# All adaLN products of a two-layer decoder moved to TensorE, in four column tiles

## The chip, the cores and the metric

One core of one Trainium2 chip runs the whole program. The metric is device time in microseconds (us), the median of the runs shown. The engines are named as in the profile: PE (TensorE; PEld is its weight load), DVE (VectorE), ACT (ScalarE), POOL (GpSimd) and SP (SyncE, which here only issues DMAs). They run side by side, each through its own instructions in order, and wait for each other by semaphores.

## What is computed

Two layers over a sequence of 512 tokens of width 1024, in float32. Each layer is a mixer (eight heads of stick-breaking attention and four heads of gated linear attention, with one input and one output projection) and a mixture of 32 experts, two for each token. Before each of the two sub-layers stands a normalisation with a shift and a scale, behind it a gate. All six vectors of a layer come from the conditioning vector `c`:

```python
c_act = jax.nn.silu(c)                                   # (1, 1024)
for l in range(DEPTH):                                   # DEPTH = 2
    mod = (c_act @ w_ada[l] + b_ada[l])[:, None, :]      # w_ada[l]: (1024, 6 * 1024)
    shift_m, scale_m, gate_m, shift_f, scale_f, gate_f = jnp.split(mod, 6, axis=-1)
    h = rms_norm(x, norm_mix[l]) * (1.0 + scale_m) + shift_m
    x = x + gate_m * hybrid_mixer(h, ...)
    h = rms_norm(x, norm_ffn[l]) * (1.0 + scale_f) + shift_f
    x = x + gate_f * hierarchical_moe(h, ...)
```

`c_act @ w_ada[l]` is a product of one row with a matrix of 24 MB. It is what the change is about.

## The kernel before

**Stages.** Mixer of layer 0, its experts (`moe`), mixer of layer 1, its experts. A planner orders the instructions of every engine from the order in which the code makes them and from what is ready; instructions made with `kept_dma` or `tc.keep_in_program_order` keep the order of the code among themselves.

**The mixer.** Its work is a list of 80 `steps`: eight projections of eight steps each (`sb_qk(0)`, `sb_v(0)`, `sb_qk(1)`, `sb_v(1)`, `gla_qk(0)`, `gla_vr(0)`, `gla_qk(1)`, `gla_vr(1)`: steps 0 to 63) and the output projection (`out_project`, `op` in the profile: steps 64 to 79). A step has three parts: `load` (SP loads weights of two steps into a `raw` slot, six steps ahead), `prep` (ACT, and POOL or DVE, split them into two rounded parts `whl`, two steps ahead; `out_project` first has POOL multiply them by `gate_m`, line 754) and `run` (12 matmuls, six in `gla_qk`). Beside the steps stand `chains`, the attention of both kinds, advanced a piece at a time, and `later`, the adaLN calls. From step 12 on `later` is given 1 turn a step in layer 0 and 0.8 in layer 1.

**The adaLN calls.** The first shift and scale of layer 0 are made at the start, by `ada` in pieces of 256 columns on PE: eight matmuls with `cs` (the activated `c`, each of its columns repeated 32 times) as the stationary operand go to four column tiles of 32, so that four partial sums stand in four groups of partitions; ACT copies them into `row`, and a matmul of each 128 columns with a column of `sel` (a one in the first row of each group) adds and transposes them. All other calls are made by `later`, 12 in layer 0 (its `gate_m`, `shift_f`, `scale_f`, `gate_f`, two halves of 512 columns each, and the shift and scale of layer 1) and 8 in layer 1. A call loads four tiles `wada` of 512 KB through the slots `raw`, of which there are four and which the projections' weights use too; then DVE does the products, one `tensor_scalar` and seven `scalar_tensor_tensor` that add a 128x512 tile times a column of `ct1` onto `row` (lines 251 and 255), in three turns. A gate is summed over the partitions by a matmul with `ones`. A shift or a scale waits for both of its halves, and then `tail` sums them (`sums`), copies the sum with ACT, writes it to DRAM and reads it back turned (`kp`), transposes it on PE (`modT`) and calls `modulation`, all in turns of its own.

**What hangs on it.** After the shift and scale of the experts (`left == 0`) `router_weights` runs: it sends two of the vectors through DRAM on POOL's queue (lines 842 and 843) and loads the router's weights there. PSUM has eight banks: four `acc` for projections, three `att` for attention, and one `misc`, in which the transposes of keys and queries (`kT`, `qT`), the attention values (`pv`), the gates and the adaLN sums take turns.

Of the kernel before, what the change touches and what calls it, by code (L numbers as in the profile page):

```python
# [9 lines left out]
F = mybir.dt.float32  # L10
# [5 lines left out]
OP = mybir.AluOpType  # L16
# [3 lines left out]
D, S, L = 1024, 512, 2  # L20
P = 128
NT, KT = S // P, D // P
# [7 lines left out]
def hybrid_decoder_kernel(ctx, tc, x, c, w_ada, b_ada, norm_mix, norm_ffn, w_in, w_gk2, b_gk, q_gain,  # L30
# [30 lines left out]
    def bank(name, tag, bufs, shape=None):  # L61
        return psum[1].tile(shape or [P, 512], F, name=name, tag=tag, bufs=bufs)
# [10 lines left out]
    def mm(o, a, b, start, stop):  # L73
        T.matmul(o, a, b, start=start, stop=stop, skip_group_check=True)  # L74
# [11 lines left out]
    def kept_dma(eng, o, a):  # L86

        tc.keep_in_program_order(eng.dma_start(o, a))
# [59 lines left out]
    glam = const.tile([P, P], F, name="glam")  # L148
    V.tensor_scalar(glam, jp, 0.0, None, op0=OP.is_ge)
    V.memset(glam[0:64, 64:128], 0.0)  # L150
    sel = ints[:, 896:1024].bitcast(F)
    V.memset(sel, 0.0)
    for j in range(4):
        V.memset(sel[32 * j:32 * j + 1, :], 1.0)
# [44 lines left out]

    log_exp()  # L200

    cs = ints[:, 640:896].bitcast(F).rearrange("p (k m) -> p k m", k=KT)
    ct1 = const.tile([P, KT], F, name="ct1")
    A.activation(ct1, cT, AF.Exp, scale=-1.0)
    A.activation(ct1, ct1, AF.Ln, bias=1.0)
    A.activation(ct1, ct1, AF.Exp, scale=-1.0)
    tc.keep_in_program_order(V.tensor_tensor(ct1, ct1, cT, op=OP.mult))
    V.tensor_copy(cs, ct1[:, :, None].to_broadcast([P, KT, 32]))

    xs = dram.tile([S, D], F, name="xs")  # L210
    xg = dram.tile([S, D], F, name="xg")
# [6 lines left out]
    bgk = cols[:, 96:100]  # L218


    halves = {}

    def ada(l, c0, n, raw, bank, at, tails=None):


        vec, half = c0 // D, c0 % D // 512
        src = w_ada[l].rearrange("(p k) n -> p k n", k=KT)
        ws, m = {}, 1024 // n
        for k in range(0, KT, m):
            w = raw([P, m, n], name="wada")  # L230
            (kept_dma if tails is None else lambda e, *a: e.dma_start(*a))(SY, w, src[:, k:k + m, c0:c0 + n])
            for i in range(m):
                ws[k + i] = w[:, i]
        yield
        row = rowt[at]([P, n], name="row")
        if tails is None:
            ps = bank("ada")
            for k in range(KT):
                mm(ps[32 * (k % 4):32 * (k % 4) + 32, 0:n], cs[:, k, :], ws[k], k < 4, k >= 4)
            A.copy(row, ps[:, 0:n])  # L240
            yield
            ps = bank("adaT")
            for i in range(n // P):
                mm(ps[:, i:i + 1], row[:, P * i:P * i + P], sel[:, 0:1], i == 0, True)
            modulation(l, vec, slice(c0 % D // P, (c0 % D + n) // P), ps)
            yield
            return
        if vec in (2, 5) and not half:
            gates[l, vec] = (gts if vec == 5 else gms[l])([P, D])
            kept_dma(G, gates[l, vec], along(b_ada, l * 6 * D + vec * D, D))  # L250
        V.tensor_scalar(row, ws[0], ct1[:, 0:1], None, op0=OP.mult)
        for k in range(1, KT):
            if k % 3 == 0:
                yield
            V.scalar_tensor_tensor(row, ws[k], ct1[:, k:k + 1], row, op0=OP.mult, op1=OP.add)  # L255
        yield
        if vec in (2, 5):
            ps = bank("adaT")
            mm(ps, ones, row, True, True)
            g = gates[l, vec][:, 512 * half:512 * half + 512]  # L260
            V.tensor_tensor(g, ps, g, op=OP.add)
            yield
        elif half:
            tails.append(tail(l, vec, [halves.pop((l, vec)), row], bank))
        else:
            halves[l, vec] = row

    def modulation(l, vec, k, ps):

# [3 lines left out]
        if scale:  # L273
            V.scalar_tensor_tensor(m, m, 1.0, norm_r[:, ffn, l, k], op0=OP.add, op1=OP.mult)
            V.tensor_scalar(m, m, math.sqrt(D), None, op0=OP.mult)

    def tail(l, vec, rows, bank):

        ps = bank("sums")
        for h in range(2):  # L280
            mm(ps[64 * h:64 * h + 64], ones[:, 0:64], rows[h], True, True)
        A.copy(rows[1], ps)
        v = dram.tile([2, 512], F, name=f"sums{l}{vec}")
        G.dma_start(v, rows[1][0::64])
        yield
        kp = const.tile([KT, P], F, name="kp", tag="kp")
        G.dma_start(kp, v.rearrange("h (k p) -> (h k) p", p=P))
        yield
        yield
        ps = bank("modT")  # L290
        T.transpose(ps[:, 0:KT], kp, ident[0:KT, 0:KT])
        modulation(l, vec, slice(0, KT), ps)
        yield


    def square(ss, xt, tt, q):
# [13 lines left out]
    def mixer(l, xt, ss, x_src, pool, later):  # L310
# [20 lines left out]
        first = {}  # L331
        if l == 0:
            for k in range(0, KT, 2):
                first[k] = [ada(l, vec * D + P * k, 256, mixs, misc, l) for vec in (1, 0)]
# [476 lines left out]
        for i, (weight, _, _, run) in enumerate(steps):  # L811
            while n_load < min(len(steps), i + ahead_load):
                steps[n_load][1]()
                n_load += 1
            while n_prep < min(len(steps), i + ahead_prep + 1):
                steps[n_prep][2]()
                n_prep += 1
            run()
            credit += weight
            while chains and credit >= 2:  # L820
                credit -= 2
                advance()
            if not chains:
                credit = 0
            if i >= 12:
                paid += 0.8 if l else 1
                while paid >= 1:
                    paid -= 1
                    next(later, None)
# [506 lines left out]
    for l in range(L):  # L1336
        if l:
            psum_pool(f"psum_mixer{l}")
        with tc.tile_pool(name=f"mixer{l}", bufs=1, reuse_waits="tile") as pool:
            raw = slots(pool, "raw", 4, 4096)  # L1340

            def later(s2, l=l, raw=raw):
                tails, left = [], 2
                for ll, j in [(l, j) for j in range(4, 12)] + [(l + 1, j) for j in range(4) if l + 1 < L]:
                    for _ in ada(ll, 512 * j, 512, raw, misc, l, tails):
                        yield
                        if tails and next(tails[0], "end") == "end":
                            tails.pop(0)
                            left -= 1
                            if left == 0:  # L1350
                                router_weights(l, s2)
                for t in tails:
                    yield from t

            xt, ss = mixer(l, xt, ss, x[0] if l == 0 else xs[:, :], pool, later)
            dump(f"mix{l}", xt[0])
        if stop == f"mixer{l}":
            return
# [33 lines left out]
```

## Time and profile before

| | |
|---|---|
| median of 3 runs | 1281.69 us (1280.89 to 1292.82) |
| profiled execution, time | 1283.96 us |
| its span, first to last instruction | 1282.1 us |
| mean granted TensorE clock | 0.969 of 2.4 GHz |
| first mixer | about 10 to 380 us |
| second mixer | about 670 to 980 us |
| instructions | 16510 |

The profile is of one execution. "Busy" is the time in which an engine had at least one instruction under way; on PE instructions overlap, so a group's mean duration is longer than the time from one start to the next. A wait is put down to the instruction whose semaphore came last. L255 is line 255 of the kernel. An `f32` matmul stands as two instructions in the trace, one on rounded (`fp32r`) parts as one.

### The profile page before, as it was taken

How to read it: one execution, taken by the hardware profiler on the slowest of the kernel's cores; microseconds unless marked ns; L12 is line 12 of the kernel's file. 1: busy time of each engine (PE TensorE's matmuls, PEld its weight loads, DVE VectorE, ACT ScalarE, POOL GpSimd, SP SyncE). 2: the span in 40 equal slices, each digit the busy share in tenths (PEclk: the TensorE clock that was granted, in tenths of full speed). 3: DMA queues.
4: the chain of work that ended last, by engine and by line, in shares of the span. 5: the costliest groups of instructions: out<-in, count | busy, mean ns of one | idle time of the engine just before them, and what ended most of it. 6: DMA issues, size and time to landing. Idle time of an engine off the chain costs nothing. (4 is left out here: it accounts for less than half of the span.)

```text
span 1282.1 us, 16510 instructions
## 1 busy us (share of the span) xinstructions
PE 1172.3 (91%) x5935; PEld 739.7 (58%) x5935; DVE 797.0 (62%) x1484; ACT 462.7 (36%) x922; POOL 307.0 (24%) x330
## 2 busy tenths in 40 slices
PE   4989978977998999999988999899998899999996
PEld 2677746655885444444447877667787444444443
DVE  3488969796544555555546988877655355555553
ACT  3366635553251111111124775554535111111111
POOL 2122232244212222221103212434421222112110
PEclk9989989998979999999998999999998999999999
DMA  8454675751485999999805547763158699999961
GB/s 282 149 178 129 205 188 161 233 160 55 186 342 174 390 394 392 392 392 376 325 1 175 161 127 227 169 172 129 50 217 325 219 385 399 399 392 386 387 253 67
DMA packets 106285, 312.28 MB, mean 244 GB/s; under 512 B 13176, under 2 KB 50284, under 8 KB 81624
## 3 DMA queue, kind: packets, MB, share of 16 engines
q1 hardware_dynamic: 96920, 289.62, 62.6%
q0 software_dynamic: 9280, 21.57, 4.9%
q8 instruction: 48, 0.79, 0.3%
q14 instruction: 37, 0.30, 0.1%
HBM read 311.10 MB, written 8.43 MB: 249 GB/s over the span
## 5 line engine op out<-in xcount | busy, mean ns | idle before, releaser
L74 PE MATMUL proj<-whl,hh 128*128 128x512 f32 (+2 forms) x768 | 220.6, 370 | 7.4 <-ACT whl L95 6.2
L78 PE MATMUL gu<-wgu,gT 128*64 128x512 f32 x1024 | 225.8, 593 | 0.0
L1095 DVE TENSOR_TENSOR x<-y,x 128x512 f32<-128x512 f32 x240 | 153.9, 684 | 14.1 <-PE y L78 14.1
L78 PEld LDWEIGHTS gu<-wgu,gT 128*64 128x64 f32 x1024 | 73.5, 137 | 146.1 <-issue 146.1
L74 PEld LDWEIGHTS proj<-whl,hh 128*128 128x128 f32 x768 | 135.5, 191 | 36.1 <-issue 7.7
L1088 POOL TENSOR_TENSOR olo<-o,ohi 128x512 fp32r<-128x512 f32 x60 | 76.4, 1274 | 301.8 <-ACT ohi L1087 301.8
L96 POOL TENSOR_TENSOR whl<-raw,whl 128x512 fp32r<-128x512 f32 (+2 forms) x80 | 90.0, 1128 | 238.3 <-ACT whl L95 184.4
L1050 DVE TENSOR_TENSOR hs<-hs,gu 128x256 f32<-128x256 f32 x32 | 13.5, 421 | 204.4 <-ACT hs L1049 204.4
L74 PE MATMUL proj<-whl,hl 128*128 128x512 f32 (+2 forms) x384 | 139.0, 363 | 0.1
L255 DVE SCALAR_TENSOR_TENSOR row<-wada,ct,row 128x512 f32<-128x512 f32 x140 | 119.9, 856 | 16.8 <-DMA wada<-in_w_ada_dram 15.6
L78 PE MATMUL y<-ohi,oT 128*128 128x512 f32 x240 | 116.1, 484 | 6.9 <-DVE x L1095 6.9
L78 PE MATMUL d<-wd,hT 128*64 128x512 f32 x512 | 116.9, 598 | 1.4 <-ACT hT L1059 1.4
L1028 ACT ACTIVATE gT<-g,mod 128x256 f32<-128x256 f32 x64 | 35.9, 565 | 177.3 <-DVE gT L1030 177.3
L78 PE MATMUL y<-olo,oT 128*128 128x512 f32 x240 | 94.6, 394 | 0.0
L95 ACT ACTIVATE whl<-raw 128x512 fp32r<-128x512 f32 (+2 forms) x128 | 66.2, 524 | 68.3 <-PE proj L74 36.6
L78 PEld LDWEIGHTS y<-ohi,oT 128*128 128x128 f32 x240 | 44.8, 186 | 74.8 <-DVE x L1095 45.4
L74 PEld LDWEIGHTS proj<-whl,hl 128*128 128x128 f32 x384 | 72.6, 189 | 13.4 <-issue 3.0
L1049 ACT ACTIVATE hs<-gu 128x256 f32<-128x256 f32 x32 | 12.3, 384 | 169.9 <-PE gu L78 169.9
L78 PEld LDWEIGHTS d<-wd,hT 128*64 128x64 f32 x512 | 33.9, 136 | 62.2 <-issue 59.9
L1082 DVE SCALAR_TENSOR_TENSOR o<-d,cws,gate_f 128x512 f32<-128x512 f32 x64 | 47.7, 748 | 34.9 <-PE d L78 34.9
L1087 ACT ACTIVATE ohi<-o 128x512 fp32r<-128x512 f32 x60 | 37.8, 629 | 78.9 <-DVE o L1082 78.8
L1003 POOL DMA_INDIRECT rows<-xg,idx x32 | 32.8, 1025 | 126.0 <-PE g L1022 108.9
(339 smaller groups left out, 2041.6 us busy)
## 6 DMA issues: line engine op xcount, KB each, us to landing
wgu<-in_w_gate_dram SPq DMA_DIRECT2D x64, 1024.0 KB, 7.7
wgu<-in_w_up_dram SPq DMA_DIRECT2D x64, 1024.0 KB, 10.3
wd<-in_w_down_dram SPq DMA_DIRECT2D x64, 1024.0 KB, 8.8
wada<-in_w_ada_dram SPq DMA_DIRECT2D x96, 512.0 KB, 4.3
raw<-in_w_in_dram SPq DMA_DIRECT2D x80, 256.0 KB, 3.6
raw<-in_w_out_dram SPq DMA_DIRECT2D x16, 512.0 KB, 3.7
raw<-in_w_in_dram SPq DMA_DIRECT2D x32, 128.0 KB, 2.9
xg<-xn POOLq DMA_DIRECT2D x8, 512.0 KB, 2.9
```

Source lines behind the costliest of these rows:

```text
L74: T.matmul(o, a, b, start=start, stop=stop, skip_group_check=True)
L78: tc.keep_in_program_order(T.matmul(o, a, b, start=start, stop=stop, skip_group_check=True))
L95: A.activation(hi, src, AF.Copy)
L96: eng.tensor_tensor(lo, src, hi.bitcast(F), op=OP.subtract)
L255: V.scalar_tensor_tensor(row, ws[k], ct1[:, k:k + 1], row, op0=OP.mult, op1=OP.add)
L1003: G.indirect_dma_start(r, None, xg[:, :], bass.IndirectOffsetOnAxis(ap=idx, axis=0), bounds_check=S - 1, oob_is_err=False)
L1028: A.activation(o, src, AF.Identity, scale=m, bias=b)
L1050: V.tensor_tensor(hs[r], hs[r], gu[r, 256:512], op=OP.mult)
L1082: V.scalar_tensor_tensor(o, pd, cws[:, i:i + 1], gate, op0=OP.mult, op1=OP.mult)
L1087: A.activation(hi, o, AF.Copy)
L1088: (G if last is None else V).tensor_tensor(lo, o, hi.bitcast(F), op=OP.subtract)
L1095: V.tensor_tensor(xc, ps, xc, op=OP.add)
```

## The change

Every adaLN call now takes the path that only the first ones took: eight matmuls in four column tiles, an ACT copy into `row`, then either a matmul with `sel` that adds the four sums into all partitions (a gate, in place of `ones`) or the one-column matmuls that add and transpose (a shift or a scale, each half by itself). `tail`, its sums, its way through DRAM and `halves` are gone. `cs` is gone as well: the stationary operand is a column of `ct1`, read 32 times with a step of zero. `sel` gets a tile of its own. A call in `later` now has five turns: three loads; the fourth load and, for a gate, the load of its bias; nothing; the matmuls and the copy; the second step. `later` is given 0.9 turns a step in layer 0 and 0.6 in layer 1, and `router_weights` is called after the call (l, 9), the last of the experts' scale.

```diff
-    sel = ints[:, 896:1024].bitcast(F)
+    sel = const.tile([P, P], F, name="sel")
...
-    V.tensor_copy(cs, ct1[:, :, None].to_broadcast([P, KT, 32]))
...
-    def ada(l, c0, n, raw, bank, at, tails=None):
+    def ada(l, c0, n, raw, bank, at, later=True):
...
             w = raw([P, m, n], name="wada")
-            (kept_dma if tails is None else lambda e, *a: e.dma_start(*a))(SY, w, src[:, k:k + m, c0:c0 + n])
+            (SY.dma_start if later else lambda *a: kept_dma(SY, *a))(w, src[:, k:k + m, c0:c0 + n])
             for i in range(m):
                 ws[k + i] = w[:, i]
+            if later and k == KT // 2:
+                yield
+        if later and vec in (2, 5) and not half:
+            gates[l, vec] = (gts if vec == 5 else gms[l])([P, D])
+            kept_dma(G, gates[l, vec], along(b_ada, l * 6 * D + vec * D, D))
         yield
+        if later:
+            yield
         row = rowt[at]([P, n], name="row")
...
+        ps = bank("ada")
+        for k in range(KT):
+            mm(ps[32 * (k % 4):32 * (k % 4) + 32, 0:n], ct1[:, k:k + 1].to_broadcast([P, 32]), ws[k], k < 4, k >= 4)
+        A.copy(row, ps[:, 0:n])
+        yield
+        if vec in (2, 5):
+            ps = bank("adaG")
+            mm(ps, sel, row, True, True)
+            g = gates[l, vec][:, 512 * half:512 * half + 512]
+            V.tensor_tensor(g, ps, g, op=OP.add)
+        else:
             ps = bank("adaT")
             for i in range(n // P):
                 mm(ps[:, i:i + 1], row[:, P * i:P * i + P], sel[:, 0:1], i == 0, True)
             modulation(l, vec, slice(c0 % D // P, (c0 % D + n) // P), ps)
...
-        V.tensor_scalar(row, ws[0], ct1[:, 0:1], None, op0=OP.mult)
-        for k in range(1, KT):
-            if k % 3 == 0:
-                yield
-            V.scalar_tensor_tensor(row, ws[k], ct1[:, k:k + 1], row, op0=OP.mult, op1=OP.add)
         yield
-        if vec in (2, 5):
-            ps = bank("adaT")
-            mm(ps, ones, row, True, True)
...
-    def tail(l, vec, rows, bank):
...
-                paid += 0.8 if l else 1
+                paid += 0.6 if l else 0.9
...
-                    for _ in ada(ll, 512 * j, 512, raw, misc, l, tails):
-                        yield
-                        if tails and next(tails[0], "end") == "end":
-                            tails.pop(0)
-                            left -= 1
-                            if left == 0:
-                                router_weights(l, s2)
-                for t in tails:
-                    yield from t
+                    yield from ada(ll, 512 * j, 512, raw, misc, l)
+                    if (ll, j) == (l, 9):
+                        router_weights(l, s2)
```

## Rows read from the trace of the kernel before

**Rows 1.** The page, part 1: busy time, share of the span, instructions.

```profile
PE 1172.3 (91%) x5935; PEld 739.7 (58%) x5935; DVE 797.0 (62%) x1484; ACT 462.7 (36%) x922; POOL 307.0 (24%) x330
```

**Rows 2.** Stretches (us): length, busy time of each engine, PE clock, DMA share, GB/s.

```profile
81.00:298.00 217.00, 185.21 (x931) 140.35 (x931) 183.28 (x306) 113.08 (x233) 66.38 (x74) 0.94 0.59 176
298.00:362.00 64.00, 60.03 (x322) 46.85 (x323) 37.80 (x65) 22.74 (x48) 17.13 (x11) 0.97 0.45 172
...
720.00:909.00 189.00, 173.75 (x921) 135.49 (x920) 155.50 (x269) 110.54 (x229) 59.07 (x64) 0.98 0.55 157
909.00:968.00 59.00, 57.71 (x323) 45.62 (x320) 34.92 (x63) 23.13 (x49) 20.00 (x11) 1.00 0.47 182
```

**Rows 3.** Chain of waits, longest pieces: start us, us, what, instructions.

```profile
778.46 2.02 PE proj L74 x16
...
795.44 1.08 PE sums L74 x4
...
835.65 1.30 PE z L74 x10
...
928.11 10.91 PE op L74 x48
...
1019.72 6.92 PE gu L78 x32
...
1036.44 6.92 PE gu L78 x32
```

**Rows 4.** Chain of waits from 720 to 909 us, shares by line.

```profile
by line: PE proj L74 15.8%; DVE row L255 9.5%; DMA wada<-in_w_ada_dram 7.4%; DMA raw<-in_w_in_dram 7.0%; PE z L74 4.8%; DVE sl L96 4.8%; issue 4.3%; DVE whl L96 4.2%; DVE t L542 3.6%; DVE t L540 2.7%; DVE two L504 2.2%; DVE ql L519 1.9%; AC
```

**Rows 5.** Timeline, 280 to 299 us: start, us, engine, line, what, [idle before].

```profile
280.61 3.24 POOL L754 TENSOR_TENSOR raw<-raw,gate_m 128x1024 f32<-128x1024 f32 x1 [7.70 <-DVE row L255]
...
285.99 2.91 DVE L255 SCALAR_TENSOR_TENSOR row<-wada,ct,row 128x512 f32<-128x512 f32 x1
...
288.95 1.97 PE L74 MATMUL sums<-row,ones 128*64 128x512 f32 x2 [5.93 <-DVE row L255]
...
292.92 4.74 DVE L726 TENSOR_TENSOR gr<-ob,gr 128x512 f32<-128x512 f32 x1
```

**Rows 6.** DVE by line, 60 to 320 us, then 700 to 980: busy, mean ns, idle before.

```profile
L255 DVE SCALAR_TENSOR_TENSOR row<-wada,ct,row 128x512 f32<-128x512 f32 x84 | 75.2, 896 | 11.2 <-DMA wada<-in_w_ada_dram 10.5
...
L251 DVE TENSOR_SCALAR row<-wada,ct 128x512 f32<-128x512 f32 x12 | 6.4, 531 | 3.5 <-PE sums L74 2.0 <-DMA wada<-in_w_ada_dram 1.5
...
L255 DVE SCALAR_TENSOR_TENSOR row<-wada,ct,row 128x512 f32<-128x512 f32 x56 | 44.6, 797 | 5.6 <-DMA wada<-in_w_ada_dram 5.1
...
L251 DVE TENSOR_SCALAR row<-wada,ct 128x512 f32<-128x512 f32 x8 | 4.1, 507 | 3.4 <-PE sums L74 2.4 <-DMA wada<-in_w_ada_dram 1.1
```

**Rows 7.** Timeline from 33 to 38 us, the first adaLN calls on PE.

```profile
33.67 0.64 PE L74 MATMUL ada<-wada,ints 128*32 128x256 f32 x8
34.24 0.73 PE L74 MATMUL proj<-whl,hh 128*128 128x512 f32 x2
...
36.55 0.61 PEld L74 LDWEIGHTS adaT<-ints,row 128*128 128x128 f32 x4
...
37.09 0.19 PEld L74 LDWEIGHTS proj<-whl,hh 128*128 128x128 f32 x1
...
37.29 0.16 DVE L272 TENSOR_TENSOR mod<-adaT,cols 128x2 f32<-128x2 f32 x1 [3.53 <-PE adaT L74]
```

**Rows 8.** Line 843 (`router_weights`): what its engine waited for, us, times.

```profile
  DMA mod<-mod: 36.7, 4
```

**Rows 9.** Timeline from 170 to 174 us: a key transpose and its readers.

```profile
170.88 0.60 PE L508 MATMUL kT<-ident,two 128*128 128x128 f32 x4
...
171.52 0.69 ACT L510 ACTIVATE ks<-kT,gain 128x512 fp32r<-128x512 f32 x1 [2.10 <-PE kT L508]
...
172.90 0.76 DVE L511 SCALAR_TENSOR_TENSOR ks<-kT,gain,ks 64x512 fp32r<-64x512 f32 x1
```

**Rows 10.** Timeline of SP's DMA issues from 155 to 190 us.

```profile
159.51 7.04 SPq L231 DMA_DIRECT2D wada<-in_w_ada_dram  x4
166.99 9.12 SPq L421 DMA_DIRECT2D raw<-in_w_in_dram  x4
```

**Rows 11.** Waits, 60 to 320 us: engine, line, for what, us, times, longest.

```profile
PEld qT L515 <- DVE ks L511: 6.8, 5, 3.6
...
PE proj L74 <- ACT whl L95: 6.6, 3, 5.9
```

More of the change, by code (lines that the diff above doesn't have):

```diff
@@ L200, in hybrid_decoder_kernel @@
     log_exp()
-    cs = ints[:, 640:896].bitcast(F).rearrange("p (k m) -> p k m", k=KT)
     ct1 = const.tile([P, KT], F, name="ct1")
@@ L218, in hybrid_decoder_kernel @@
     bgk = cols[:, 96:100]
-    halves = {}
-    def ada(l, c0, n, raw, bank, at, tails=None):
+    def ada(l, c0, n, raw, bank, at, later=True):
         vec, half = c0 // D, c0 % D // 512
@@ L230, in ada @@
             w = raw([P, m, n], name="wada")
-            (kept_dma if tails is None else lambda e, *a: e.dma_start(*a))(SY, w, src[:, k:k + m, c0:c0 + n])
+            (SY.dma_start if later else lambda *a: kept_dma(SY, *a))(w, src[:, k:k + m, c0:c0 + n])
             for i in range(m):
                 ws[k + i] = w[:, i]
+            if later and k == KT // 2:
[3 more added lines that the diff above has]
+            kept_dma(G, gates[l, vec], along(b_ada, l * 6 * D + vec * D, D))
         yield
+        if later:
+            yield
         row = rowt[at]([P, n], name="row")
[L236 to L240, printed above, removed]
-            yield
+        ps = bank("ada")
[9 more added lines that the diff above has]
+        else:
             ps = bank("adaT")
@@ L245, in ada @@
             modulation(l, vec, slice(c0 % D // P, (c0 % D + n) // P), ps)
-            yield
[L247 to L250, printed above, removed]
-        V.tensor_scalar(row, ws[0], ct1[:, 0:1], None, op0=OP.mult)
-        for k in range(1, KT):
-            if k % 3 == 0:
-                yield
-            V.scalar_tensor_tensor(row, ws[k], ct1[:, k:k + 1], row, op0=OP.mult, op1=OP.add)
-        yield
-        if vec in (2, 5):
-            ps = bank("adaT")
-            mm(ps, ones, row, True, True)
[L260 to L266, printed above, removed]
+        yield
     def modulation(l, vec, k, ps):
@@ L275, in modulation @@
             V.tensor_scalar(m, m, math.sqrt(D), None, op0=OP.mult)
-    def tail(l, vec, rows, bank):
[L279 to L293, printed above, removed]
     def square(ss, xt, tt, q):
@@ L333, in mixer @@
             for k in range(0, KT, 2):
-                first[k] = [ada(l, vec * D + P * k, 256, mixs, misc, l) for vec in (1, 0)]
+                first[k] = [ada(l, vec * D + P * k, 256, mixs, misc, l, False) for vec in (1, 0)]
             xt = [xq([P, 2, D], name="x") for _ in range(2)]
@@ L1342, in later @@
             def later(s2, l=l, raw=raw):
-                tails, left = [], 2
                 for ll, j in [(l, j) for j in range(4, 12)] + [(l + 1, j) for j in range(4) if l + 1 < L]:
-                    for _ in ada(ll, 512 * j, 512, raw, misc, l, tails):
-                        yield
-                        if tails and next(tails[0], "end") == "end":
-                            tails.pop(0)
-                            left -= 1
-                            if left == 0:
-                                router_weights(l, s2)
-                for t in tails:
-                    yield from t
+                    yield from ada(ll, 512 * j, 512, raw, misc, l)
+                    if (ll, j) == (l, 9):
+                        router_weights(l, s2)
             xt, ss = mixer(l, xt, ss, x[0] if l == 0 else xs[:, :], pool, later)
```

## The prediction

> **What bounds the kernel now.** The page comes first. TensorE (PE) is busy for 91% of the span and VectorE (DVE) for 62% [rows 1], but the change touches only the two mixers, so the split by stretch is what counts. I cut each mixer after its second projection, where the attention work begins, and where the output projection begins: 81 to 298 us and 298 to 362 us in layer 0, 720 to 909 us and 909 to 968 us in layer 1 [rows 2]. In the first stretch of each layer PE and DVE are both 82 to 92% busy. In the second PE is at 94 to 98% and DVE at 59%.
>
> PE's busy share overstates its work, because matmuls overlap their neighbours. The chain of waits shows what one costs in a dense run: 48 output-projection instructions in 10.91 us (0.227 us each), 16 of 272 columns in 2.02 us (0.126 us), 10 scores in 1.30 us (0.13 us) [rows 3]. After the second projection each layer runs 384 projection instructions of 512 columns, 96 of 272, and the rest (931 - 480 = 451 in layer 0, 921 - 480 = 441 in layer 1). So layer 0 needs 384 x 0.227 + 96 x 0.126 + 451 x 0.13 = 158 us of its 217 us, a density of 0.73; layer 1 needs 156 of 189 us, 0.83. The output projection of layer 0 needs 192 x 0.227 + 130 x 0.13 = 60.5 of 64 us, 0.95. PE therefore has real holes exactly where the adaLN products run on DVE.
>
> The chain says who makes them. It reaches back to 673 us, so it covers layer 1: of 720 to 909 us DVE's `row` products (L255) hold 9.5%, 18.0 us, and waits for their loads 7.4%, 14.0 us [rows 4]. In layer 0 the same thing is seen directly: at 280 us GpSimd (POOL) has waited 7.70 us behind a `row` product before it can scale a `w_out` tile, that same stretch has a `row` product of 2.91 us and a `gr` product of 4.74 us on DVE, and PE stands 5.93 us before it can sum a row [rows 5]. The granted clock falls to 0.94 on the mean of that stretch [rows 2].
>
> **The change, part by part.**
>
> *Removed from DVE.* 12 calls in layer 0 and 8 in layer 1, each one L251 and seven L255: 75.2 + 6.4 = 81.6 us and 44.6 + 4.1 = 48.7 us [rows 6], 130 us in all. DVE's share of the first stretches falls from 84 and 82% to about half; it stops being a bound. The extra small operations (`modulation` runs twice a vector instead of once) are 12 of about 0.16 us [rows 7], 2 us, hidden in that idle time.
>
> *Added to PE, the products.* A call has 8 matmuls, each two instructions, in four column tiles. The nearest row is the 256-column version at the start of layer 0, where half a call (8 instructions) begins at 33.67 us and the next matmul at 34.24, 0.57 us later [rows 7]. Above: twice the columns, two halves, 4 x 0.57 = 2.28 us. Below: `gu`, 512 columns in two column tiles, does 32 instructions in 6.92 us [rows 3], 0.43 us a pair, so four tiles would do 16 in 4 x 0.43 = 1.73 us. I take 2.0 us, midway, since one row has the right width and the other the right tiles. 20 x 2.0 = 40 us. The row already shows four tiles side by side; the Trainium skill, page "TensorE: Matmul & The Clock Gate", section "Measured speedup vs the span model", is less kind: its four-tile packing gained 3.07 times and not 4, which would make the 1.73 a 2.25 (an estimate), 5 us more in the sum than mine. No row here has 512 columns in four tiles.
>
> *Added to PE, the second step.* A shift or scale half transposes by four one-column matmuls, 8 instructions. Four take 0.54 us from weight load to the next one's (36.55 to 37.09) [rows 7]; so 1.1 us, 12 times, 13 us. A gate half keeps its sum by a matrix of ones, now `sel`: nothing. Removed: six times the sums of two rows, 1.08 us each [rows 3], 6.5 us. PE in all: 12 x 2.0 + 8 x 1.1 - 4 x 1.08 = 28.5 us more in layer 0 and 8 x 2.0 + 4 x 1.1 - 2 x 1.08 = 18 us more in layer 1.
>
> *ScalarE (ACT)* copies one 128x512 row a call; a 128x512 copy of its takes 0.69 us [rows 9]: 14 us, less six that go. It idles 104 of the 217 us [rows 2]: nothing. *The DRAM round trips* of the sums (12 small DMAs on POOL) go; POOL is at 31% there, and what stalls it is another round trip, that of `router_weights`, 36.7 us in four waits [rows 8], which stays: nothing. *Bytes loaded* are the same. *`cs` and `sel`* at the start: nothing, DVE's constants have no reader in a hurry.
>
> *Moved.* A call now takes 5 turns instead of 4 or 5, at 0.9 and 0.6 turns a step instead of 1 and 0.8. Turns begin at step 12 of 80, so the calls end at step 12 + 60/0.9 = 12 + 40/0.6 = 79 in both layers, against 12 + 52/1 = 64 and 12 + 36/0.8 = 57 now. So some two calls in each layer run inside the output projection (steps 64 to 79), and `router_weights` of layer 1, which comes after 30 turns, starts at step 62 instead of 50. There the POOL queue holds the scaling and splitting of `w_out` behind its wait, and the `w_out` loads share four `raw` slots with `wada`. Below: nothing. Above: one such POOL wait a layer, 9 us each [rows 8], 18 us. I take 4 us: POOL is busy for only 20 of 59 us there [rows 2].
>
> *The sum.* PE's need becomes 158 + 28.5 = 186.5 us and 156 + 18 = 174 us. Packed without a hole, the stretches would shrink by 30.5 and 15 us: -46 us is what PE allows. I take the density that PE reaches in layer 0 where no product stands on DVE, 0.95 [rows 2, 3]: 186.5/0.95 = 196 (-21) and 174/0.95 = 183 (-6), together -27 us; with the 4 us above, -23 us. The holes close only if the density rises from today's 314/406 = 0.77 over both stretches; the change breaks even at 360.5/406 = 0.89. The check from the other side: the `row` products held 18 us of layer 1's chain; PE's 18 us in their place, on the chain for half of the time, leave -9 us there. The MoE stages stay as they are, one pair of experts in 16.72 us [rows 3]; they start earlier. The profiled execution took 1283.96 us, so 1261 us; the median of the runs, 1281.69, is 2.3 us lower, so the forecast is 1258.7 us, **1259 us**.
>
> **The rivals.**
>
> *The products were the bound, one for one (more is gained).* If the chain's share holds for layer 0 as well, products and their loads hold 32 us in layer 1 and, with 12 calls for 8, 48 us in layer 0; half of PE's 46 us comes back: -57 us, 1225 us. For it: the stalls of [rows 5], where DVE and POOL lengthen each other. The Trainium skill, page "SBUF — State Buffer", section "Who interferes with whom", says that a DVE instruction with two SBUF inputs and a GpSimd one that reads SBUF exclude one another; the `row` products are of that kind, and the row of 4.74 us agrees. Against: PE allows only 46 us.
>
> *One PSUM bank becomes the bound (within 1%).* `misc` is a single bank for the key and query transposes, the attention values, gates and adaLN. A call takes it twice now, a non-gate call took it once on average: 20 takes more, each held as a key transpose holds it, from 170.88 to 173.66 us, 2.8 us [rows 9]. If PE waits 0.6 us at each of 40 takes, 24 us, the gain is gone: 1283 us. The Trainium skill, page "TensorEngine Tiling (Array Packing)", section "PSUM Bottleneck", warns of this: tiling speeds the matmul, not the emptying of PSUM. Against: the order is planned around the bank, and the longest such wait of today, of `qT` on the readers of `kT`, comes to 6.8 us over 260 us of layer 0 [rows 11].
>
> *The weight stream starves (slower).* A call holds all four `raw` slots until its matmuls run, while DVE freed them one after another. The input weights come through the same slots and the same SyncE queue: today one set of four loads took 9.12 us to issue behind `wada` tiles, and PE stood 5.9 us for the split of its weights [rows 10, 11]. Break-even is 23/20 = 1.15 us a call; at 2.5 us a call, 50 us against -23 us: 1309 us. Against: one long stall in 20 calls so far; for it: DVE's absorbing queue is gone, and a PE that waits for the fourth tile holds everything behind it.
>
> That the tiles don't run side by side is excluded by [rows 7].
>
> **How the numbers follow.** A measurement here tells 1% from no change, 13 us: faster is below 1269, slower above 1294. Forecast 0.54 (1240 to 1269), more gained 0.13, one bank 0.20, starved stream 0.13. Faster 0.67, same 0.20, slower 0.13. The range leaves out the far half of the first rival and the last one: 1228 to 1283 us.
>
> **What would show it.** Right: no `row` work on DVE; 320 `ada` instructions more, their sets of 16 near 2.0 us; the stretches of 217 and 189 us shorter by some 20 and 6 us; PE's idle time no longer ended by DVE `row`. Wrong: waits of `kT`, `qT` or `ada` on readers of the `misc` bank; `proj` waiting for the split of `raw` tiles after long issues on SyncE; `op` waiting on POOL in layer 1; sets of 16 near 7 us.

## The result, and the profile after

The changed kernel takes 1343.88 us (median of 4 runs, 1339.21 to 1346.17) against 1283.1 us beside it: ratio 1.0461, interval 1.0416 to 1.0506. It is slower by 60 us, where 1259 us was forecast. The profiled execution took 1339.21 us with a span of 1337.4 us, 55.3 us more than the span of before; its mean granted clock is 0.966, that of before 0.969.

The page after, part 1 (busy, share, instructions), the costliest line of the moved products in part 5 (busy, mean ns, idle before and what ended it), and three rows of part 6 (KB, median us from issue to landing):

```profile
PE 1225.2 (92%) x6321; PEld 753.0 (56%) x6321; DVE 687.6 (51%) x1335; ACT 467.0 (35%) x936; POOL 292.3 (22%) x318
...
L74 PE MATMUL ada<-wada,ct 128*32 128x512 f32 (+1 forms) x448 | 69.6, 566 | 11.9 <-DMA wada<-in_w_ada_dram 8.8
...
raw<-in_w_in_dram SPq DMA_DIRECT2D x80, 256.0 KB, 4.2
raw<-in_w_out_dram SPq DMA_DIRECT2D x16, 512.0 KB, 5.5
...
xg<-xn POOLq DMA_DIRECT2D x8, 512.0 KB, 11.2
```

Against [rows 1] DVE is busy for 109 us less and PE for 53 us more. What is new is idle time of PE that ends with the landing of a `wada` tile.

The four stretches of [rows 2], cut at the same instructions (end of the second projection, first and last output projection), in the same columns:

```profile
78.00:303.00 225.00, 205.48 (x1098) 144.13 (x1097) 114.10 (x214) 113.54 (x236) 53.44 (x63) 0.96 0.48 142
303.00:377.00 74.00, 69.99 (x386) 49.13 (x385) 39.19 (x69) 24.23 (x51) 21.75 (x13) 1.00 0.43 143
743.00:938.00 195.00, 184.17 (x1031) 139.04 (x1031) 109.86 (x208) 111.59 (x233) 49.59 (x57) 0.99 0.43 130
938.00:1014.00 76.00, 69.51 (x356) 48.72 (x357) 38.94 (x66) 23.43 (x50) 23.25 (x14) 0.96 0.40 131
```

The stretches grew by 8, 10, 6 and 17 us; DVE's share fell from 84 and 82% to 51 and 56% in the first stretches, and these did not get shorter. Another 14 us lie behind the mixers, between their last output projection and the next steady work (318.9 to 324.5 us in layer 0, 314.3 to 323.1 us in layer 1).

The SP queue's issues of after, in layer 1 (start us, us from the first to the last of a group, what, how many):

```profile
853.95 24.50 SPq L226 DMA_DIRECT2D wada<-in_w_ada_dram  x4
886.87 4.55 SPq L391 DMA_DIRECT2D raw<-in_w_in_dram  x8
...
914.47 1.40 SPq L716 DMA_DIRECT2D raw<-in_w_out_dram  x3
917.89 27.04 SPq L226 DMA_DIRECT2D wada<-in_w_ada_dram  x3
950.18 0.37 SPq L716 DMA_DIRECT2D raw<-in_w_out_dram  x1
964.58 0.37 SPq L226 DMA_DIRECT2D wada<-in_w_ada_dram  x1
965.42 1.39 SPq L716 DMA_DIRECT2D raw<-in_w_out_dram  x3
```

Three `wada` loads now spread over 27 us where [rows 10] has four in 7.04 us, the fourth follows at 964.58 us, and the weights of the output projection get slots one to three at a time between them. The expert weights stand behind all this in the same queue. The chain of waits of after shows what that does at the end of the mixer (start us, us, what):

```profile
1003.12 27.21 issue
...
1036.52 11.68 DMA xg<-xn
```

The first expert load goes out at 1003.57 us, 11 us before the mixer ends (933.2 us in the kernel before, 35 us before it), so its 1 MB loads run beside the write of `xg`, which takes 11.2 us instead of 2.9 (medians of eight).

### The profile page after: what moved, and what is told of

It is laid out like the page before. It is cut to its first block, busy times and chain, and to the rows that moved or that the text cites. A ratio compares the mean times of both kernels' runs of the same rounds, so it can differ in the third digit from the quotient of the medians.

```text
span 1337.4 us, 17099 instructions
## 1 busy us (share of the span) xinstructions
PE 1225.2 (92%) x6321; PEld 753.0 (56%) x6321; DVE 687.6 (51%) x1335; ACT 467.0 (35%) x936; POOL 292.3 (22%) x318
## 5 line engine op out<-in xcount | busy, mean ns | idle before, releaser
L96 POOL TENSOR_TENSOR whl<-raw,whl 128x512 fp32r<-128x512 f32 (+2 forms) x80 | 85.3, 1069 | 306.5 <-ACT whl L95 258.0
L74 PE MATMUL ada<-wada,ct 128*32 128x512 f32 (+1 forms) x448 | 69.6, 566 | 11.9 <-DMA wada<-in_w_ada_dram 8.8
L78 PEld LDWEIGHTS d<-wd,hT 128*64 128x64 f32 x512 | 34.0, 137 | 62.1 <-issue 59.9
L992 PE MATMUL g<-ident,rows 128*128 128x128 f32 x256 | 50.4, 292 | 19.7 <-DMA rows<-xg,idx 18.9
## 6 DMA issues: line engine op xcount, KB each, us to landing
wgu<-in_w_up_dram SPq DMA_DIRECT2D x64, 1024.0 KB, 11.2
xg<-xn POOLq DMA_DIRECT2D x8, 512.0 KB, 11.2
```

Source lines behind the costliest of these rows:

```text
L78: tc.keep_in_program_order(T.matmul(o, a, b, start=start, stop=stop, skip_group_check=True))
L96: eng.tensor_tensor(lo, src, hi.bitcast(F), op=OP.subtract)
L992: tc.keep_in_program_order(T.transpose(ps[:, at:at + P], r[:, P * k:P * k + P], ident))
```

## The experiments

Two theories. **A, slots:** a call holds four of four `raw` slots until its 16 matmuls run, so the input and output weights, which use the same slots, come late. **B, PE itself:** the products are too much for a PE that had fewer holes than the forecast saw; or what costs is the landing of the last tile, on which PE stands in its order. In the tables a layer is summed from its first projection (layer 0: from the start) to the end of its output projection, and the MoE part follows to the next layer or the end.

### What the products cost without their loads, and what everything else costs

Without loads and slots, the same PE instructions read a constant:

```diff
-            w = raw([P, m, n], name="wada")
-            (SY.dma_start if later else ...)(w, src[:, k:k + m, c0:c0 + n])
...
+            if later:
+                mm(o, ct2[:, k:k + 1].to_broadcast([P, 32]), ident[:, None, :].to_broadcast(...), k < 4, k >= 4)
...
```

> The kernel after, but the calls of the mixers' later part load nothing and take no weight slot: their 16 instructions run on the identity tile instead (so the modulation is not that of the reference, and the experts chosen may differ). TensorE's work, the PSUM bank, the copies and the turns are as in the kernel after. Theory 2 (slots and loads): the first stretches, 225 and 195 us, fall to about 200 and 182, the output projections to 66 and 62, the whole to about 1275. Theory 1 (late calls): the output projections and the gaps behind them improve, because no slot is held late, the first stretches stay within 5 us; about 1305. Theory 3 (TensorE's time): within 10 us of the kernel after.

> As e2_noload, but the products, copies and second steps of these calls are left out as well; the gates keep their biases and shift and scale are made from the biases alone (not the reference's values). This is the mixer with neither engine doing the products. It gives TensorE's floor in the first stretches: by the prediction's sum 158 and 156 us; if the rest of the mixer has waits of its own, more. Theory 2: e2_noload minus this run is close to the 46 us of TensorE work. Theory 3: e2_noload minus this run is 70 us or more.

Measured: 1283.61 us without the loads, 1224.95 us without the products (one run each).

| span, us | layer 0 | MoE 0 | layer 1 | MoE 1 | sum |
|---|---|---|---|---|---|
| before | 361.5 | 318.9 | 287.4 | 314.3 | 1282.1 |
| after | 377.4 | 324.5 | 312.4 | 323.1 | 1337.4 |
| no loads | 343.3 | 319.0 | 303.3 | 316.1 | 1281.7 |
| no products | 317.5 | 322.5 | 267.3 | 315.6 | 1222.9 |

So the products with their loads cost 44.0 us in layer 0 and 20.1 us in layer 1 on DVE, and the calls on PE 25.8 and 36.0 us with no load to wait for. Without its loads the change is a wash (+0 us); the other 56 us of the spans come with the loads. In layer 1 the eight calls cost twice what their own instructions take on PE, some 18 us (an estimate from the sets and transposes below). Some 8 us of the rest go with the granted clock, if PE is taken as the bound (again an estimate): it was 0.96 and 0.97 in the two stretches of that layer without the loads, 0.99 and 1.00 without the products. Another 4.7 us are a stall behind POOL (shown in the part on the prediction). The last 5 us stay open. The two first stretches without products, in the windows' columns:

```profile
90.00:258.00 168.00, 163.35 (x905) 132.16 (x904) 117.32 (x202) 109.25 (x227) 51.41 (x57) 0.99 0.25 77
...
680.80:848.30 167.50, 162.84 (x901) 131.79 (x900) 113.81 (x197) 108.89 (x227) 48.22 (x52) 0.99 0.25 77
```

PE is busy for 97% of them: with no adaLN products at all these stretches take 168 us. The moved products have about the size forecast. One set of 16 and one transpose, from the PE timeline of the run without loads (start us, us, what, instructions):

```profile
176.16 1.92 PE L74 MATMUL ada<-ident,ct 128*32 128x512 f32 x16
178.01 0.50 PE L74 MATMUL proj<-whl,hh 128*128 128x512 f32 x1
...
178.87 0.97 PE L74 MATMUL adaT<-sel,row 128*128 128x1 f32 x8
179.70 0.36 PE L74 MATMUL z<-sh,n 128*128 128x256 f32 x1
```

The next instruction starts 1.85 us after the set's first (2.0 forecast) and 0.83 us after the transpose's (1.1 forecast).

### When the calls run

```diff
-                paid += 0.6 if l else 0.9
+                paid += 1.0 if l else 1.2
```

> The kernel after with one edit: the adaLN calls get 1.2 turns a step in layer 0 and 1.0 in layer 1 instead of 0.9 and 0.6, so that the last of them ends at about step 62 and 52 of 80, before the output projection, instead of at step 79. Theory 1 (late calls: work inside the output projection, slots held there, and expert weights that start to load late): the output projections, 75 and 77 us in the kernel after, go back to about 64 and 59, and the gaps up to the experts shrink by some 15 us in both layers together; 1343 falls to about 1300. Theory 2 (the four weight slots are held by the adaLN tiles, so the projections' weights come late, whenever the calls run): the calls only get denser in the first stretches, what the output projection gains is lost there; about 1330 to 1345. Theory 3 (it is TensorE's time for the products, wherever they run): no change, 1335 to 1345.

Measured: 1350.65 us (1.0527, 1.0482 to 1.0571). The output projections return to 59.9 and 58.7 us and the MoE parts to 319.4 and 315.6 us, so the late calls did cost there what the profile showed; but the first stretches, into which the calls were pushed, lose 25 and 30 us. In this run the place of the calls decides only where the loss is paid; no theory had the 1350 us in its range.

### Half calls, tight calls, empty calls

Calls of 256 columns hold two slots (their turns at 0.96 and 1.44 a step, so that they end at the same step); tight calls ask for all four tiles in one turn and run the matmuls in the next; empty calls hold four slots but load 64 bytes a partition:

```diff
-                for ll, j in [(l, j) for j in range(4, 12)] + ...:
-                    yield from ada(ll, 512 * j, 512, raw, misc, l)
+                for ll, j in [(l, j) for j in range(8, 24)] + ...:
+                    yield from ada(ll, 256 * j, 256, raw, misc, l)
```

```diff
+        if later:
+            yield
+            yield
...
-            if later and k == KT // 2:
-                yield
...
-        if later:
-            yield
         row = rowt[at]([P, n], name="row")
```

```diff
-            (SY.dma_start if later else ...)(w, src[:, k:k + m, c0:c0 + n])
+            if later:
+                SY.dma_start(w[:, :, 0:8], src[:, k:k + m, c0:c0 + 8])
...
```

> The kernel after with calls of 256 columns instead of 512, twice as many: each loads two tiles and holds two of the four weight slots until its matmuls have run, instead of four. Turns (four a call, 24 and 16 calls) at 1.44 and 0.96 a step, so the last call ends at step 79 as in the kernel after. The products cost 0.57 us a half set instead of 1.85 us a set of twice the columns: about 0.4 us more a pair, 9 us in all, and the copies double. Theory 2 (slots): the first stretches shrink by 20 us and more, in all 1343 to about 1315. Theory 1 (late calls): no gain, 1340 to 1350. Theory 3: 9 us more, 1350.

> The kernel after with one thing moved: a call gives its two empty turns first, then issues its four loads in one turn, the matmuls in the next, the second step in the turn behind it (five turns as before, the same pace). Its tiles are asked for after the weights of the steps in between, so each slot should be held for about one turn instead of three. Theory A (the cost of the loads is the time for which the four slots are held): a good part of the 60 us that e2_noload gave back, 20 us or more: below 1325. Theory B (it is the loading itself, bytes and landing times): the matmuls come sooner behind their loads and wait longer for them: 1343 or more.

> The kernel after, calls with all four slots taken and held as in it, but each load brings only 8 of 512 columns of two rows (64 bytes a partition instead of 4 KB), and the matmuls read these 8 columns 64 times over, by a small stationary operand, so TensorE's work is the same (the modulation is not the reference's, the experts chosen may differ). Theory A (slots): the loads still wait for slots and keep the weights of the projections out; the first stretch of layer 0 stays near 220 us, the whole near 1325 to 1340. Theory B (bytes, landing): as e2_noload, about 1285 to 1295.

Measured: half calls 1309.06 us (1.0213, 1.0167 to 1.0259), 35 us less than after; tight calls 1348.78 us (1.0521, 1.0449 to 1.0592), no gain, which missed theory A's expectation and met theory B's; empty calls 1320.89 us (one run), so 23 of the 60 us go with the bytes and 37 stay while calls of four loads share four slots.

Why the tight calls missed shows when loads and products are put in order. A `wada` tile holds its slot from its issue to the end of the last product that reads it. The table has the mean hold, the time in which all slots are `wada`'s, the calls whose last load is issued after the call's first product has begun, and the sets of 16 in which other matmuls run between the products of the last load and the rest:

| kernel | slots | mean hold, us | all slots `wada`'s, us | last load behind first product | last products apart | time, us |
|---|---|---|---|---|---|---|
| before | 4 | 9.1 | 1 | 20 of 20 | (on DVE) | 1283.1 |
| after | 4 | 15.9 | 31 | 12 of 20 | 14 of 20 | 1343.9 |
| calls earlier | 4 | 12.2 | 19 | 16 of 20 | 17 of 20 | 1350.7 |
| tight calls | 4 | 10.7 | 4 | 18 of 20 | 19 of 20 | 1348.8 |
| empty calls | 4 | 15.4 | 31 | 12 of 20 | 11 of 20 | 1320.9 |
| half calls | 4 | 12.1 | 0 | 0 of 40 | 3 of 40 | 1309.1 |

Neither the hold nor the time with all slots taken goes with the loss: tight calls have the shortest hold of the changed kernels and all slots taken for 4 us, and are as slow as any. What goes with it is the last load. The weights use the four slots too, and so a call's fourth tile often gets its slot only when the call's own first tile has been read. One call of after (start us, us, what):

```profile
140.67 1.91 PE L74 MATMUL ada<-wada,ct 128*32 128x512 f32 x12
141.59 0.37 SPq L226 DMA_DIRECT2D wada<-in_w_ada_dram  x1
145.36 1.05 PE L74 MATMUL ada<-wada,ct 128*32 128x512 f32 x4 [0.35 <-DMA wada<-in_w_ada_dram]
```

PE goes through three tiles in 1.84 us (to the next matmul's start) and through the fourth, when it has landed, in 0.98 us: 2.82 us in all where an unbroken set takes 1.85. In the kernel before, the last load is behind the first product in every call, but there DVE takes 0.8 to 0.9 us for a product [rows 6] and has four more to do on the two tiles between; what it still waited for its loads came to 15.6 us over all calls [rows 6].

### More slots

The room for a fifth slot came from slots whose loss is tested by itself in the first of these runs. Six slots take one `sh`/`sl` slot and one `w` slot more, and the kernel before with five gives up one `sh`/`sl` and one `s2` slot; these losses were not tested by themselves. The edit for five:

```diff
-        raw = slots(pool, "raw", 4, 4096)
+        raw = slots(pool, "raw", 5, 4096)
-        s2 = slots(pool, "s2", 4, 2048)
+        s2 = slots(pool, "s2", 3, 2048)
-        rowt[l] = slots(pool, "row", 2, 2048)
+        rowt[l] = slots(pool, "row", 1, 2048)
...
```

> The changed kernel with the slots of adaLN rows cut from 2 to 1 and those of small work tiles (s2) from 4 to 3: the room that the next two runs need, given up for nothing. Both theories: 1340 to 1365 us, since a row is copied and used within a few us and s2 tiles live as briefly. It is what the next two are measured against.

> The same, with a fifth raw slot in the room given up. Theory A, the four tiles of a call keep the input and output weights out of the four shared slots (37 of the 60 us stayed when the bytes went but the slots were held): at least 15 us below the run before it, because one slot is always left to the weights, and the issues of four wada tiles that took 20 to 30 us shorten to below 15. Theory B, what costs is the landing of the tiles and TensorE waiting in its order for the fourth: within 8 us of the run before it.

> Six raw slots (room also from one sh/sl slot and one w slot). Theory A: at least 30 us below the control, near 1300 us, since the weights have two slots of their own, as many as one pair of their tiles needs; the loads of expert weights start earlier than 10 us before the mixer's end again. Theory B: within 10 us of the control.

> The kernel before with five raw slots (room from one sh/sl slot and one s2 slot). Theory A: VectorE frees the tiles one after another, mean hold 15.1 us with little waiting of PE behind it, so little is gained: 1265 to 1290 us. Theory B: 1278 to 1290 us, no change. If it falls below 1265, the slots bound the kernel before as well.

Measured, side by side: the control 1340.76 us (1.0484, 1.0378 to 1.059), five slots 1310.77 us (1.025, 1.0143 to 1.0357), six slots 1307.62 us (1.0225, 1.012 to 1.0331), the kernel before with five slots 1288.02 us (1.0037, 0.9998 to 1.0077). One slot is worth 30 us to the changed kernel, and the kernel before gains nothing, as far as the slots that it gave up cost it nothing. With five and with six slots the products of the last load run apart in none of the 20 calls, where the control has 14. Between the control and five slots the span falls by 33 us (1340.2 to 1306.9): 12 us of it at the moved sets (their time up to the next matmul, and PE's idle time ahead of them: 64.9 and 52.7 us), 12 us behind the mixers (651.4 and 639.6 us in the two MoE parts), the rest elsewhere in the mixers. The SP issues with six slots, at the place shown above:

```profile
892.08 8.53 SPq L716 DMA_DIRECT2D raw<-in_w_out_dram  x3
900.69 1.45 SPq L226 DMA_DIRECT2D wada<-in_w_ada_dram  x3
914.07 0.37 SPq L716 DMA_DIRECT2D raw<-in_w_out_dram  x1
928.18 0.37 SPq L226 DMA_DIRECT2D wada<-in_w_ada_dram  x1
```

The three `wada` loads that spread over 27.04 us go out in 1.45 us. With six slots the weights land sooner again, and the write of `xg` comes part of the way back:

```profile
raw<-in_w_in_dram SPq DMA_DIRECT2D x80, 256.0 KB, 3.1
raw<-in_w_out_dram SPq DMA_DIRECT2D x16, 512.0 KB, 3.8
...
xg<-xn POOLq DMA_DIRECT2D x8, 512.0 KB, 6.2
```

Theory A holds for this half of the loss in that the slots decide it, and both of its bounds (15 and 30 us under the control) were met. But it is not that a call keeps all four slots; its last load has to wait for one. The 3 us of the sixth slot can't be told from nothing, and 24 us over the run without loads were left.

### What six slots leave

> Calls of 256 columns, two slots each, with six raw slots: four are left to the weights. If the slots were all of the cost of the loads, six slots would have removed it; they leave about 24 us over the run without loads (1283.6). Rival 1, the rest is still slots (a call of 512 columns holds four of six for some 17 us): this run falls to 1280 to 1295 us. Rival 2, the rest is the order, PE standing where a call's last tile lands late and products that are not yet there: 1300 to 1312 us, as with six slots and calls of 512 columns, since every load still lands just before its matmuls.

> Six raw slots and loads of 64 bytes a partition in place of 4 KB; the products run on PE on that little, so their result is left out. With four slots the same cut of the bytes brought 1343.9 to 1320.9 us, 23 us less. Rival 1, slots: they are held for almost as long, so 1300 to 1308 us, no change against six slots with all bytes. Rival 2, landing and bytes: what six slots left (24 us) goes with the bytes, 1280 to 1292 us.

Both edits are those above, with six slots. Measured: half calls 1315.34 us (1.0278, 1.0211 to 1.0345), empty calls 1291.13 us (1.0096, 1.0066 to 1.0126). Fewer slots a call bring nothing more, which speaks against slots as the rest; without the bytes 16.5 of the 24 us go. The two causes nearly add up:

| us | four slots | six slots |
|---|---|---|
| full loads | 1343.9 | 1307.6 |
| 64 bytes a partition | 1320.9 | 1291.1 |

Slots are worth 36 us with the bytes and 30 without; the bytes 23 and 16. Where the bytes are paid is mostly layer 0: 363.3 us with six slots, 350.4 with six and no bytes. The longest stall there with six slots is one of 6.45 us (start us, us, what):

```profile
208.43 1.39 SPq L226 DMA_DIRECT2D wada<-in_w_ada_dram  x3
209.92 0.93 SPq L391 DMA_DIRECT2D raw<-in_w_in_dram  x2
219.83 0.60 PE L636 MATMUL kd<-ident,gk 128*128 128x128 f32 x4
226.46 0.42 ACT L95 ACTIVATE whl<-raw 128x256 fp32r<-128x256 f32 x1 [7.29 <-DMA raw<-in_w_in_dram]
227.19 0.56 ACT L638 COPY kt<-kd 128x512 f32<-128x512 f32 x1
227.81 3.64 PE L74 MATMUL ada<-wada,ct 128*32 128x512 f32 x16 [6.45 <-ACT kt L638]
```

PE stands at a set here not for its tiles but for the `misc` bank, which `kd` fills. ACT should empty it, but stands ahead of that for an input weight that was issued right behind three `wada` loads and landed 16.2 us later. With six slots and no bytes the load in the same place lands after 3.7 us, and the stall is not there. So bytes of `wada` are paid, in this one stall at least, as a late input weight. Half calls with six slots measured 8 us over whole calls with six, which the two intervals don't tell apart.

### Only the gate calls on PE

In the kernel before, the gate halves' products were moved to PE and the rest left on DVE, in both layers and in layer 0 alone:

```diff
+        if vec in (2, 5) and l == 0:
+            yield
+            ps = bank("ada")
+            for k in range(KT):
+                mm(ps[32 * (k % 4):32 * (k % 4) + 32, 0:n], ct1[:, k:k + 1].to_broadcast([P, 32]), ws[k], k < 4, k >= 4)
+            A.copy(row, ps[:, 0:n])
...
```

> As e8_mix0, with the gate calls of both layers on TensorE. Layer 1 had 21 us above its floor with 8 calls on VectorE; with 4 there and 4 on TensorE it would lose about 4 x 2.8 = 11 us to TensorE and gain about half of the 21: equal to e8_mix0 within 5 us. If TensorE's time counts in full and VectorE's calls cost nothing in layer 1, 11 us more than e8_mix0.

> The kernel before, in which the four gate calls of layer 0 alone run on TensorE in four column tiles (loads in one turn, matmuls two turns later), the other 16 calls on VectorE as before; pace as before. Sel gets a tile of its own, and the small tile kp moves into the slot junk to make room. If the floors that e3_nocalls gave (168 us a stretch) are right, layer 0 has 49 us above its floor in the kernel before and layer 1, with 8 calls on VectorE, 21 us: layer 0 with 8 calls on VectorE and 4 on TensorE would come to 168 + 21 + 4 x 2.8 = 200 us instead of 217, and the whole to about 1267. If slots decide (theory A), the four TensorE calls hold theirs longer and give some of it back: 1270 to 1280. If VectorE's calls don't stand in the way of anything, 1282 or more.

Measured: both layers 1304.9 us (1.0181, 1.0113 to 1.0249), layer 0 alone 1281.83 us (0.9995, 0.9957 to 1.0033), no gain where 1267 us were expected for layer 0 alone; both layers lost 23 us against that run, where at most 11 were expected. Layer 0 shortens by 2.5 us only; layer 1 takes 309.5 us with its four calls on PE against 287.4, in keeping with a PE that has no room there, though what share its loads have in these 22 us was not measured. No version that was run beats the kernel before. By the tables, half calls with six slots in layer 0 alone would leave 4 us (358.6 + 317.5 against 361.5 + 318.9); that is below what can be told here, and it was not run.

## Why the prediction was wrong

*Removed from DVE: right in the main.* No `row` product is left on DVE and its share of the first stretches fell to about half. DVE's busy time fell by 109 us, where 130 us less some 2 were forecast.

*Sizes on PE: right, where the set is unbroken.* Without loads the next matmul starts 1.85 us after a set (2.0 forecast) and 0.81 to 0.91 us after a transpose (1.1). That 14 of the 20 sets would be broken was not forecast. The Trainium skill, page "TensorE: Matmul & The Clock Gate", section "Measured speedup vs the span model", has a packing of four row tiles gain 3.07 times; the four tiles here are column tiles. By that figure a set would have taken 2.25 us (the estimate in the forecast); here it takes 1.85, nearer to the 1.73 us worked out from the two-tile rows [rows 3], and the measurement decides.

*The holes of PE: the first step that failed.* The forecast took PE's need from the cost of instructions in dense runs, 156 us of 189 in layer 1, and read 33 us of holes. The run without products shows 167.5 us for that stretch, with PE busy for 162.84. Of the 11 us that the need was too small, 5 are the 384 projection instructions of 512 columns (from each one's start to the next start, idle gaps left out, they take 92.4 us, 0.241 each, where the forecast had 0.227 from the longest dense run), and 5 are idle time of PE that stays with no products at all (4.7 us). In the kernel before PE stood idle for 15.3 us in that stretch. So layer 1 could hide about 10 us of what it got, and with the loads taken out of the way it still lost 15.9 us (303.3 against 287.4) where -6 was forecast: 4.5 in this stretch, 9.4 in the output projection, which took two calls' products on a PE that was busy for 98% [rows 2], 2 ahead of both. The 4.5 us are about the stall behind POOL shown below. What misled was the density of before: time in which PE's instructions run slower than in the longest dense run was counted as holes.

Layer 0 gained 18.2 us (343.3 against 361.5), near the -21, but that is in part luck. The granted clock in its two stretches was 0.94 and 0.97 before [rows 2] and 0.98 and 1.00 in the run without loads; in layer 1 it was 0.98 and 1.00 before and 0.96 and 0.97 there. With PE as the bound these differences come to some 10 us of the gain and 6 of the loss (an estimate). Whether the change moved the clock, one run can't tell; the two layers together, +0 us where -27 was forecast for them, do not depend on it, since the mean clock of the two executions is 0.969 and 0.970.

*Edits costed at nothing, and the 4 us for the moved calls: wrong, and the larger miss.* This is the rival of the starved weight stream, which had a chance of 0.13 and a price of 1309 us (2.5 us a call). It happened, at 60 us in 20 calls, 3.0 us a call: 30 to 36 us go with a fifth and sixth slot, 16 to 23 us with the bytes, and both together come within 8 us of the run without loads. The mechanism is in part another than the rival's: all four slots are `wada`'s for 31 us in the whole run. PE, like DVE, frees a tile as soon as its products are done; but it is through three tiles in 1.84 us, and the fourth, whose load waits for one of their slots, lands some 4 us later. "One long stall in 20 calls so far" was no argument against that, since the slow products of DVE kept the same order of loads away from PE in all 20 calls. "a PE that waits for the fourth tile", named there for the rival, is what the trace shows.

What PE waited for in layer 0's first stretch (us in total, times, longest):

```profile
PE proj L74 <- POOL whl L96: 9.4, 2, 6.0
PE ada L74 <- DMA wada<-in_w_ada_dram: 3.8, 6, 1.5
...
PEld proj L74 <- POOL whl L96: 10.2, 2, 6.4
PEld ada L74 <- DMA wada<-in_w_ada_dram: 7.3, 7, 2.0
```

Summed from their starts to the next start on PE, the 20 moved sets of after take 56.4 us, and PE stands idle ahead of them for 11.2; without loads it is 38.0 and 0.4 us, with six slots 39.8 and 7.3, and these 7.3 end with ACT's copy of `kt`, as shown above, not with a landing. So 29 us of the 60 are lost at the sets, 9 us of them with six slots. The waits on the split of the weights (`whl`) are no proof of the slots: the run without loads has them too, and they come from POOL.

What the forecast did not see at all is the step behind: the expert weights queue after the last `wada` loads and run beside the `xg` write, 14 us in the two transitions. With six slots the two MoE parts are back at 319.2 and 316.3 us.

*POOL, costed at nothing: wrong by some 9 us.* The round trip of `router_weights` through DRAM stays, as forecast, but PE, which did not wait behind it before, now does. From the run without loads (start us, us, what):

```profile
165.21 0.57 POOL L821 DMA_DIRECT2D mod<-mod  x1 [8.77 <-DMA mod<-mod]
...
168.63 1.97 POOL L96 TENSOR_TENSOR whl<-raw,whl 128x256 fp32r<-128x256 f32 x2
169.43 0.80 PE L74 MATMUL proj<-hh,whl 128*128 128x512 f32 x1 [4.40 <-POOL whl L96]
```

POOL stands for 8.8 us, and the split that PE needs is made only behind that. Layer 1 has the same at 835 us, 4.7 us of PE. In after such waits on `whl` come to 13.6 us in both mixers, in the kernel before to 0.9. The run without products has none, as its `router_weights` of both layers runs in the first 40 us, so these 9 us are part of what PE's products seem to cost; that moving the round trip would give them back was not tested.

*One PSUM bank: not what happened.* The run without loads takes the `misc` bank as often as the changed kernel, and there `ada`, `adaT` and `adaG` wait for readers of the bank for 2.5 us in all, where the rival had 24. With six slots it is 10 us, 6.4 of them in the one stall shown above, whose origin is a late weight. The Trainium skill, page "TensorEngine Tiling (Array Packing)", section "PSUM Bottleneck", warns that the copy out of PSUM may bound a tiled matmul; no run here shows it.

*The products as the bound: half right.* On DVE they and their loads cost 64 us in the mixers. Taking them off DVE is worth that; with the products on PE the mixers pay 62 us before a byte is loaded, some 9 of them for POOL's round trip.

*The break-even.* The 1.15 us a call that the weight stream was allowed to cost rested on 23 us of gain. With nothing gained on PE it lay at zero.

## What to carry to other kernels

Before work moves from a slow reader to a fast one, look at when the last load of each group is issued. If it waits for a slot that the group's own first tile holds, a slow reader hides its landing behind the tiles between, and a fast one stands at it or is broken in two; where other loads use the same slots, one slot more can decide it (30 us here). And take the room on the engine that gets the work from its idle gaps in the trace, not from its instruction count times the best spacing: an engine busy for 92% of a stretch had at most 8% to give.

## What was not expected of the hardware

The write of `xg` (512 KB on POOL's queue, median of eight) takes 2.9 us in the kernel before, 4.8 us without the loads, 6.2 us with six slots and 11.2 us in the changed kernel. The first of the 1 MB expert loads goes out 35, 41, 23 and 11 us before the mixer's end in layer 1, so the longest writes are those with the loads on top of them: the same transfer takes nearly four times as long in that company. In the run with the calls earlier, where the expert loads go out 35 us ahead again, it takes 4.8 us. That the company is the cause was not tested by itself.
